# Late modulation columns of a hybrid mixer block: products in column groups of the array in place of sums on the vector engine

## The chip, the cores and the metric

The kernel runs on one core of one Trainium2 chip. A core has five engines that run side by side, each through its own list of instructions in order: TensorE (PE in the profile; its weight loads are shown apart as PEld), VectorE (DVE), ScalarE (ACT), GpSimd (POOL) and SyncE (SP), which here mostly issues DMAs. TensorE writes its results to PSUM, eight banks of 128 partitions by 2 KB; everything else lives in SBUF or in HBM. The metric is the time of one execution on the device in microseconds; lower is better. Beside the timed runs there is one profiled execution, from which all rows of the trace come.

## The reference, cut to what matters

One layer of a diffusion backbone on a latent stream of 1024 tokens by 1024 channels, with a context of 256 tokens. All inputs and the output are float32. A vector `c` of 1024 numbers is turned into six modulation vectors of 1024 numbers, and these scale, shift and gate the stream:

```python
mod = jax.nn.silu(c) @ w_mod[l] + b_mod[l]                    # (1024) @ (1024, 6144)
sh1, sc1, g1, sh2, sc2, g2 = jnp.split(mod[:, None, :], 6, axis=-1)
h = x * (1.0 + sc1) + sh1
z = h @ w_in_l                                                # one input projection, four head groups
y_a = mlstm_mixer(...); y_b = sgu_mixer(...); y_c = conv_mixer(...); y_d = s5_mixer(...)
y = jnp.concatenate([y_a, y_b, y_c, y_d], axis=-1) @ w_out[l]
x = layer_norm(ALPHA * x + g1 * y, ln1_w[l], ln1_b[l])
x = layer_norm(ALPHA * x + g2 * swiglu(x * (1.0 + sc2) + sh2, w_ffn_in[l], w_ffn_out[l]), ln2_w[l], ln2_b[l])
```

The case is about g1, sh2 and sc2, which are columns 2048 to 5119 of `w_mod`: 3072 dot products of length 1024. They are needed late: g1 at the output projection, sh2 and sc2 after the first layer norm.

## The kernel before, in words

The program is written as a straight sequence of operations on tiles. Tiles come from pools; a tile's tag names a slot (or a ring of slots) that tiles share one after another, and a tile can take its slot only when the one before it has been read for the last time. When the program is built, a planner puts the instructions of each engine in one fixed order: what is written earlier goes first, unless a model of durations says that it would have to wait, in which case later work that is ready is put ahead. A few operations are marked as of high priority. On the chip each engine then keeps to its list; an instruction that waits holds up all behind it on its engine, and a DMA that waits for its slot holds up the DMAs behind it on SP's list.

The stages are, in the order written: sh1 and sc1 and the modulated streams; the S5 mixer; projections for the other mixers, each as three passes of a split float32 product (line 884, and line 893 with 256 columns); the mLSTM mixer, whose states (line 487) and eight chunks (lines 531 to 578) pass small products between TensorE, ScalarE and VectorE; the convolution's taps, a long list of VectorE operations (lines 673 to 681); the gating mixer (lines 647 to 653); the convolution's norms (lines 691 to 702); the output projection in two halves of 512 tokens (line 1184); the first layer norm with transposes (line 1204); and the feed-forward layer in seven products of half size instead of eight (lines 1345 and 1470), which takes the second half of the time. Splits of weights into two parts take ScalarE (line 854) and VectorE (line 855).

The six groups of 512 late columns come from `mod_late` (line 975): groups 0 to 2 are written after the first half of the mLSTM, groups 3 to 5 after the first half of the output projection. For a group, `mod_acc` (line 962) loads eight tiles of 128 rows by 512 columns of `w_mod` (line 966, on SP's list), and VectorE adds each, scaled by the matching entry of silu(c) per partition, to an accumulator of 128 partitions by 512 (lines 970 and 968). That leaves one partial sum per partition. Four float32 products of the accumulator with a column of ones (line 981) add over the partitions and put the 512 results into a 128x4 block, to which the bias is added (line 982). The PSUM bank for it is the one bank of tag c, which the gating mixer and the convolution's norms use too. In groups 0 to 2 the accumulator takes the slot of tag kxc, and the weight tiles go in turn through the slots vxc and mw; kxc and vxc are free once the mLSTM's states are made. In groups 3 to 5 the accumulators take kxc and vxc, and the weight tiles go through four parts of the slot vx, which is free after the last mLSTM chunk.

The results of groups 0 and 1 become g1 (lines 1119 to 1125), spread over all partitions by a product; those of groups 2 to 5 are sh2 and sc2 (line 1137 and lines 1219 to 1221). g2 has its own sum (line 1254) and is not touched.

Of the kernel before, what the change touches and what calls it, by code (L numbers as in the profile page):

```python
# [9 lines left out]
F32 = mybir.dt.float32  # L10
# [4 lines left out]
MUL, ADD, SUB, MAX, MIN = ALU.mult, ALU.add, ALU.subtract, ALU.max, ALU.min  # L15
# [4 lines left out]
def bc(ap, shape):  # L20
    return ap.to_broadcast(shape)
# [684 lines left out]
D = 1024  # L706
# [14 lines left out]
def layout(x):  # L721

    f = np.ascontiguousarray
    g = {n: f(x[n]) for n in ("x", "w_mod", "b_mod", "ln1_w", "ln1_b", "ln2_w", "ln2_b", "mlstm_gate_bias", "s5_glu_w")}
    g["cst"] = const_table()
    kp = lambda a: a.reshape(-1, 128).T
    g["cols"] = f(np.concatenate([kp(x["c"]), kp(x["c_ctx"])] + [kp(x[src][0])[:, k0:k0 + nk] for _, src, k0, nk in VEC], 1))

    st = lambda a: a[0].reshape(2, 8, 2, 64).transpose(2, 3, 0, 1).reshape(128, 16)
    ldt = np.broadcast_to(x["s5_log_dt"][0][:, :, None], (2, 16, 64))[None]  # L730
    bt = [x["s5_b_" + n][0].reshape(8, 2, 64, 16).transpose(1, 2, 0, 3).reshape(128, 128) for n in ("re", "im")]
    ct = [x["s5_c_" + n][0].reshape(8, 2, 16, 64).transpose(1, 3, 0, 2).reshape(128, 128) for n in ("re", "im")]
    dk = np.zeros((128, 8), np.float32)
    dk[0:32] = x["s5_d"][0].reshape(8, 32).T
    g["s5p"] = f(np.concatenate([st(x["s5_a_re"]), st(x["s5_a_im"]), st(ldt)] + bt + ct + [dk], 1))
    g["conv_t"] = f(x["conv_w"][0].reshape(31, 2, 128).transpose(2, 1, 0))
    g["sgu_wt"] = f(x["sgu_w"][0].transpose(2, 0, 1))
    g["sgu_bb"] = f(np.repeat(x["sgu_b"][0].reshape(2, 2, 128).transpose(1, 0, 2), 64, 0))
    g["xt"], g["ct"] = (f(x[n][0].T.reshape(8, 128, -1).transpose(1, 0, 2)) for n in ("x", "ctx"))
    tile_ = lambda w: w.reshape(-1, 128, w.shape[1]).transpose(1, 0, 2)  # L740
    half = lambda w: f(np.stack([tile_(w[0:512]), tile_(w[512:1024])]))
    wi = x["w_in"][0]
    g["wt"] = f(np.stack([tile_(wi[:, c:c + 128]) for _, c in TCOLS]))
    g["wk"], g["wb"] = half(wi[:, 256:512]), half(wi[:, 1296:1552])
    g["wv"] = half(np.concatenate([wi[:, 512:768], wi[:, 1024:1040]], 1))
    g["wm"] = f(x["w_mod"][0][:, 0:2 * D].reshape(4, 2, 128, 2, 2, 512).transpose(4, 0, 2, 1, 3, 5))
    blocks = lambda w: f(w.reshape(8, 128, -1, 128).transpose(2, 1, 0, 3))
    g["w1"] = blocks(x["w_ffn_in"][0])
    g["wo"] = f(x["w_out"][0].reshape(4, 2, 128, 2, 512).transpose(3, 0, 2, 1, 4))
    g["w2"] = f(x["w_ffn_out"][0].reshape(NFF // 2, 2, 128, 2, 512).transpose(1, 3, 2, 0, 4).reshape(4, 128, NFF // 2, 512))  # L750
    g["w2k"] = f(x["w_ffn_out"][0].reshape(NFF // 2, 2, 128, 2, 512).transpose(0, 2, 1, 3, 4).reshape(NFF // 2, 128, 4, 512))
    return g
# [10 lines left out]
def body(tc, A, out):  # L763
    nc = tc.nc
    v, a, pe, gp = nc.vector, nc.scalar, nc.tensor, nc.gpsimd
    e = Env()
    e.nc, e.tc = nc, tc
    st = ExitStack()
    with st:
        cp = st.enter_context(tc.tile_pool(name="const", bufs=1))  # L770
# [9 lines left out]
        ld = nc.sync.dma_start  # L780
# [22 lines left out]
        ccol = cp.tile([128, 16], F32, name="ccol")  # L803
# [7 lines left out]
        mx = tc.alloc_tile_pool(name="mx", bufs=1, side="right")  # L811
# [135 lines left out]
        kxc = mx.tile([128, 2, 256], F32, name="kxc", tag="kxc")  # L947
# [14 lines left out]
        def mod_acc(acc, wt, c0):  # L962
            n = acc.shape[-1]
            for k in range(8):
                w = wt()
                ld(w, wm[k * 128:(k + 1) * 128, c0:c0 + n])
                if k:
                    v.scalar_tensor_tensor(acc, w, ccol[:, k:k + 1], acc, op0=MUL, op1=ADD)
                else:
                    v.tensor_scalar(acc, w, ccol[:, k:k + 1], None, op0=MUL)  # L970
# [1 line left out]

        m2c = cp.tile([128, 24], F32, name="m2c")

        def mod_late(groups, acc_, wt, tag):
            for i in groups:
                acc = acc_()
                mod_acc(acc, wt, (4 + i) * 512)
                ps = e.ps(tag)
                for j in range(4):  # L980
                    pe.matmul(ps[:, j:j + 1], lhsT=acc[:, j * 128:(j + 1) * 128], rhs=e.one, start=True, stop=True)
                v.tensor_tensor(m2c[:, i * 4:i * 4 + 4], ps[:, 0:4], col["b2"][:, i * 4:i * 4 + 4], op=ADD)


# [32 lines left out]
        for j in range(2):  # L1017
            ps = ps_mm()
# [78 lines left out]
        def sgu_half(hf):  # L1097
# [3 lines left out]
        chunks(0)  # L1101
        y["a"] = latT(page2([128, 2, 1024]), "o", AF.Sigmoid)
        norms(0)
        mq = iter(range(99))
        mod_late(range(0, 3), lambda: mx.tile([128, 512], F32, name="macc", tag="kxc"),
                 lambda: mx.tile([128, 512], F32, name="mw", tag=("vxc", "mw")[next(mq) % 2]), "c")

        y["b"] = latT(page2([128, 2, 1024]), "u", AF.Gelu_apprx_tanh)
        gv = page2([128, 8, 256])
# [103 lines left out]
        out_proj(0)  # L1213
        mw = mx.tile([128, 4, 512], F32, name="vx", tag="vx")
        ms = iter(range(32))
        ma = iter(("kxc", "vxc") * 2)
        mod_late(range(3, 6), lambda: mx.tile([128, 512], F32, name="macc", tag=next(ma)), lambda: mw[:, next(ms) % 4], "c")

        v.scalar_tensor_tensor(s2, sc2, 1.0, col["l1w"], op0=ADD, op1=MUL)
        v.scalar_tensor_tensor(b2, sc2, 1.0, col["l1b"], op0=ADD, op1=MUL)  # L1220
# [352 lines left out]
```

## Time and profile before

| | us |
|---|---|
| median of 3 runs | 1174.7 |
| lowest, highest | 1173.6, 1176.86 |
| profiled execution | 1174.02 |
| its span, first to last instruction | 1172.2 |

Rows of the trace give times in us from the start of the span. A row of a timeline has start, duration, engine, line, operation, the tiles out<-in, the shape, and how many instructions of that kind are merged (x12); what stands in brackets is idle time just ahead of it, and what ended it. For a product the shape is rows\*columns of the stationary operand, then partitions x columns of the moving one. The duration of a product reaches to its modelled end, and products overlap, so the pace is read from one start to the next. A row of who waited for whom has the total wait in us and how many times. A row of busy time by stretch has the length, then the busy us and count of PE, PEld, DVE, ACT and POOL, the granted clock of TensorE as a share of full speed, the share of the DMA engines, and GB/s.

### The profile page before, as it was taken

Reading aid. Unit: us, or ns where it says so; the run is one execution under the profiler, and the core shown is the slowest. Engines: PE = TensorE matmul, PEld = TensorE weight load, DVE = VectorE, ACT = ScalarE, POOL = GpSimd, SP = SyncE. Lnnn points to the kernel's source line nnn. Section 1 sums busy time; section 2 is a strip of 40 time slices with the busy share of each in tenths; the row PEclk is TensorE's granted clock in tenths of the full one; section 3 lists DMA queues with packets and bytes.
Section 4 is the critical chain, followed back from the end, with each engine's and each line's share of the span. In section 5 each row is a group of like instructions: output and inputs, shape, how many; then the busy total and the mean of one; then the engine's idle time right before and its main releaser. Section 6 shows DMA issues by size and latency. Waiting matters only on the chain.

```text
span 1172.2 us, 15295 instructions
## 1 busy us (share of the span) xinstructions
PE 1133.1 (97%) x5671; PEld 895.4 (76%) x5671; DVE 930.0 (79%) x1851; ACT 445.6 (38%) x691; POOL 9.6 (1%) x30
## 2 busy tenths in 40 slices
PE   6999999999999999989999999999999999999996
PEld 1487788667888788868887888888887778888884
DVE  6588999978899889879968676777778767766775
ACT  1454444522326433582233332333232336433431
POOL 0010000000000000000000000000000000000000
PEclk9999999999999999999999999999999999999998
DMA  9542111022143346362333545345445679766621
GB/s 359 212 133 89 42 46 57 27 71 70 57 141 109 99 157 212 99 225 73 108 123 112 196 179 180 134 153 192 170 154 202 255 259 349 238 196 220 195 103 72
DMA packets 63147, 177.87 MB, mean 152 GB/s; under 512 B 5537, under 2 KB 9793, under 8 KB 61282
## 3 DMA queue, kind: packets, MB, share of 16 engines
q1 hardware_dynamic: 62658, 175.93, 43.3%
q8 instruction: 44, 0.72, 0.3%
q0 software_dynamic: 272, 0.70, 0.2%
q10 hardware_dynamic: 144, 0.29, 0.1%
q14 instruction: 29, 0.24, 0.1%
HBM read 136.54 MB, written 40.35 MB: 151 GB/s over the span
## 4 chain that ended last, share of the span: by engine, by line
PE 77%; DVE 13%; DMA 4%; issue 4%; ACT 2%; POOL 0%; DVEq 0%; ACTq 0%; POOLq 0%
PE mm L1345 16%; PE mm L884 13%; PE a L1345 8%; PE mm L1470 6%; PE mm L1184 4%; PE b L1345 4%; PE b L884 4%; PE a L1470 3%; PE b L1470 3%; PE mm L893 3%; PE c L1470 2%; PE b L564 1%; DVE whl L855 1%; DVE pg L855 1%; DMA raw<-in_w_dram 1%
## 5 line engine op out<-in xcount | busy, mean ns | idle before, releaser
L854 ACT CAST whl<-raw 128x512 fp32r<-128x512 f32 (+1 forms) x198 | 120.3, 622 | 283.2 <-PE mm L884 69.6
L884 PE MATMUL mm<-pg,whl 128*128 128x512 f32 x816 | 217.7, 406 | 1.4 <-ACT pg L1207 1.2
L1345 PE MATMUL mm<-pg,whl 128*128 128x512 f32 x864 | 205.9, 390 | 0.4 <-DVE whl L855 0.3
L1345 PEld LDWEIGHTS mm<-pg,whl 128*128 128x128 f32 x864 | 161.9, 188 | 35.6 <-issue 0.8
L884 PEld LDWEIGHTS mm<-pg,whl 128*128 128x128 f32 x816 | 147.7, 190 | 38.8 <-issue 6.1
L855 DVE TENSOR_TENSOR whl<-raw,whl 128x512 fp32r<-128x512 f32 (+1 forms) x198 | 133.6, 689 | 46.3 <-ACT whl L854 44.7
L1345 PE MATMUL a<-pg,whl 128*128 128x512 f32 x432 | 104.7, 390 | 3.6 <-ACT whl L854 3.6
L1345 PEld LDWEIGHTS a<-pg,whl 128*128 128x128 f32 x432 | 80.7, 188 | 21.3 <-ACT whl L854 4.8
L855 DVE TENSOR_TENSOR pg<-raw,pg 128x1024 fp32r<-128x1024 f32 (+1 forms) x52 | 59.6, 1149 | 20.8 <-ACT pg L854 20.7
L855 DVE TENSOR_TENSOR pg<-whl,pg 128x1024 fp32r<-128x1024 f32 (+1 forms) x42 | 47.4, 1133 | 31.9 <-ACT pg L854 31.6
L854 ACT CAST pg<-raw 128x1024 fp32r<-128x1024 f32 (+1 forms) x52 | 51.5, 992 | 48.9 <-DMA raw<-in_w_dram 18.0
L854 ACT CAST pg<-whl 128x1024 fp32r<-128x1024 f32 (+1 forms) x42 | 41.1, 980 | 65.9 <-PE c L1470 25.2
L893 PE MATMUL mm<-whl,pg 128*128 128x256 f32 (+1 forms) x448 | 63.1, 288 | 0.0
L893 PEld LDWEIGHTS mm<-whl,pg 128*128 128x128 f32 x448 | 58.1, 190 | 1.5 <-issue 1.1
L1345 PE MATMUL b<-pg,whl 128*128 128x512 f32 x216 | 51.9, 389 | 0.0
L1184 PE MATMUL mm<-pg 128*128 128x512 f32 x192 | 50.8, 409 | 0.0
L1184 PE MATMUL mm<-whl,pg 128*128 128x512 f32 x192 | 50.2, 398 | 0.3 <-DVE pg L1172 0.3
L1470 PE MATMUL mm<-pg,pg 128*128 128x512 f32 x171 | 48.0, 389 | 0.0
L1470 PE MATMUL a<-pg,pg 128*128 128x512 f32 x162 | 47.2, 390 | 0.2 <-DVE hs L1484 0.2
L1470 PE MATMUL b<-pg,pg 128*128 128x512 f32 x162 | 47.1, 389 | 0.0
L1345 PEld LDWEIGHTS b<-pg,whl 128*128 128x128 f32 x216 | 40.5, 188 | 8.4
L1184 PEld LDWEIGHTS mm<-pg 128*128 128x128 f32 x192 | 37.4, 198 | 8.6 <-DVE pg L855 0.7
(468 smaller groups left out, 1838.2 us busy)
## 6 DMA issues: line engine op xcount, KB each, us to landing
raw<-in_w_dram SPq DMA_DIRECT2D x59, 512.0 KB
gd<-pg SPq DMA_DIRECT2D x22, 1024.0 KB
whl<-gd SPq DMA_DIRECT2D x35, 512.0 KB
pg<-in_w2k_dram SPq DMA_DIRECT2D x11, 1024.0 KB
td<-pg SPq DMA_DIRECT2D x11, 1024.0 KB
raw<-td SPq DMA_DIRECT2D x20, 512.0 KB
pg<-in_wm_dram SPq DMA_DIRECT2D x16, 512.0 KB
raw<-in_wo_dram SPq DMA_DIRECT2D x16, 512.0 KB
```

What stands on the lines that cost most here:

```text
L564: pe.matmul(ps[:, x * 65:(x + 1) * 65], lhsT=D[d][:, x], rhs=vx[:, h, :], start=True, stop=True)
L854: a.copy(hi, r)
L855: v.tensor_tensor(lo, r, hi.bitcast(F32), op=SUB)
L884: pe.matmul(ps[h], lhsT=W(wi, k), rhs=rhs(hi, h, k), **f)
L893: pe.matmul(ps, lhsT=lhs(hi, k), rhs=Ws[k // 4](wi, k % 4), start=(k == 0 and n == 0), stop=(k == 7 and n == 2))
L1184: pe.matmul(ps, lhsT=Yr(hi, half, k)[:, t * 128:(t + 1) * 128], rhs=Ws[k // 2](wi, k % 2), start=(i + n == 0), stop=(i == 7 and n == 2))
L1345: pe.matmul(ps, lhsT=W[:, wi, k, :], rhs=B[b][hi][:, k], start=(first and k + n == 0), stop=(k == 3 and n == 2), skip_group_check=True)
L1470: pe.matmul(ps[t], lhsT=Ag[:, hi, k, t * 128:(t + 1) * 128], rhs=Bg[:, wi, k], start=(first and k0 + k + m == 0), stop=(k0 + k == NK - 1 a ...
```

## The change

`mod_late` no longer sums on VectorE. The weights are laid out anew on the host: `wm2[i * 4 + x, n]` holds, for column block x of 128 columns of group i, four row blocks of 128 rows (rows n \* 512 to n \* 512 + 511) side by side, so that a load is again 128 partitions by 2 KB. Each load feeds four float32 products: row block g uses its 128 entries of silu(c), repeated over 32 columns, as the stationary operand, the 128x128 weights as the moving one, and writes 32 equal rows to partitions 32g to 32g + 31 of a PSUM bank of tag c. The two loads n = 0 and 1 of a column block add up there. After eight loads the bank holds four partial sums, each repeated over 32 partitions, for 512 columns. ScalarE copies it to SBUF, and four products with the column `gsum` add over the partitions, as the ones did before. `gsum` is 1 in partitions 0, 32, 64 and 96 and 0 elsewhere, made by one VectorE operation out of the identity; it picks one of each 32 equal rows.

The weight tiles of groups 0 to 2 go in turn through kxc, vxc and mw; those of groups 3 to 5 through the four parts of vx as before. The accumulators are gone. `mod_acc` stays for g2.

```diff
@@ layout
+    g["wm2"] = f(x["w_mod"][0][:, 2 * D:5 * D].reshape(2, 4, 128, 24, 128).transpose(3, 0, 2, 1, 4))
@@ body
-        def mod_late(groups, acc_, wt, tag):
+        gsum = cp.tile([128, 1], F32, name="gsum")
+
+        def mod_late(groups, wt, tag):
+
             for i in groups:
-                acc = acc_()
-                mod_acc(acc, wt, (4 + i) * 512)
                 ps = e.ps(tag)
-                for j in range(4):
-                    pe.matmul(ps[:, j:j + 1], lhsT=acc[:, j * 128:(j + 1) * 128], rhs=e.one, start=True, stop=True)
+                for x in range(4):
+                    for n in range(2):
+                        w = wt()
+                        ld(w, A["wm2"][i * 4 + x, n])
+                        for g in range(4):
+                            pe.matmul(ps[g * 32:(g + 1) * 32, x * 128:(x + 1) * 128], lhsT=bc(ccol[:, n * 4 + g:n * 4 + g + 1], [128, 32]),
+                                      rhs=w[:, g], start=(n == 0), stop=(n == 1))
+                z = e.tmp([128, 512], "hs")
+                a.copy(z, ps)
+                ps = e.ps(tag)
+                for x in range(4):
+                    pe.matmul(ps[:, x:x + 1], lhsT=z[:, x * 128:(x + 1) * 128], rhs=gsum, start=True, stop=True)
                 v.tensor_tensor(m2c[:, i * 4:i * 4 + 4], ps[:, 0:4], col["b2"][:, i * 4:i * 4 + 4], op=ADD)
@@ groups 0 to 2
-        mq = iter(range(99))
-        mod_late(range(0, 3), lambda: mx.tile([128, 512], F32, name="macc", tag="kxc"),
-                 lambda: mx.tile([128, 512], F32, name="mw", tag=("vxc", "mw")[next(mq) % 2]), "c")
+        v.tensor_reduce(gsum, e.ident[:, 0:128:32], axis=mybir.AxisListType.X, op=ADD)
+        mq = itertools.cycle(("kxc", "vxc", "mw"))
+        mod_late(range(0, 3), lambda: mx.tile([128, 4, 128], F32, name="mw", tag=next(mq)), "c")
@@ groups 3 to 5
-        ma = iter(("kxc", "vxc") * 2)
-        mod_late(range(3, 6), lambda: mx.tile([128, 512], F32, name="macc", tag=next(ma)), lambda: mw[:, next(ms) % 4], "c")
+        mod_late(range(3, 6), lambda: mw[:, next(ms) % 4].rearrange("p (g c) -> p g c", g=4), "c")
```

## The prediction

> **What bounds the kernel now.** I read the page first, then the busy time by stage around the two places that the change touches, then TensorE's instructions in order of time there, because a busy share alone does not say whether the engine could take more.
>
> ```profile
> span 1172.2 us, 15295 instructions
> ...
> PE 1133.1 (97%) x5671; PEld 895.4 (76%) x5671; DVE 930.0 (79%) x1851; ACT 445.6 (38%) x691; POOL 9.6 (1%) x30
> ...
> PE 77%; DVE 13%; DMA 4%; issue 4%; ACT 2%; POOL 0%; DVEq 0%; ACTq 0%; POOLq 0%
> ```
>
> TensorE (PE) is the engine that is busy nearly always, and 77% of the chain that ends last runs over it. VectorE (DVE) is second. The next view is the busy time in four stretches that hold all of the late modulation.
>
> ```profile
> core 0: us, PE busy (x) PEld busy (x) DVE busy (x) ACT busy (x) POOL busy (x), PEclk, DMA share, GB/s
> 225.00:305.00 80.00, 78.82 (x515) 58.59 (x509) 67.06 (x195) 22.32 (x41) 0.54 (x1) 0.98 0.20 67
> 305.00:365.00 60.00, 59.21 (x368) 52.78 (x367) 55.91 (x117) 20.98 (x31) 0.00 (x0) 1.00 0.28 90
> 365.00:420.00 55.00, 52.58 (x366) 40.87 (x366) 45.56 (x134) 27.16 (x38) 0.00 (x0) 0.94 0.39 135
> 420.00:480.00 60.00, 59.48 (x286) 48.14 (x285) 56.92 (x104) 24.83 (x33) 0.00 (x0) 1.00 0.56 178
> ```
>
> Both engines are nearly full here: DVE 56 of 60 us in the second stretch and 57 of 60 in the fourth. Which of them sets the end is read from TensorE's rows in order of time (start, duration, engine, line, operation, tiles, shape, count).
>
> ```profile
> 318.77 9.79 PE L884 MATMUL mm<-pg,whl 128*128 128x512 f32 x42
> 328.82 0.63 PE L600 MATMUL b<-cst,msq 128*128 128x128 f32 x4 [0.26 <-DVE msq L596]
> ...
> 435.20 2.89 PE L1184 MATMUL mm<-pg 128*128 128x512 f32 x12
> 437.93 2.88 PE L1184 MATMUL mm<-whl,pg 128*128 128x512 f32 x12
> 440.65 2.88 PE L1184 MATMUL mm<-pg 128*128 128x512 f32 x12
> 443.37 2.88 PE L1184 MATMUL mm<-whl,pg 128*128 128x512 f32 x12
> 446.09 2.88 PE L1184 MATMUL mm<-pg 128*128 128x512 f32 x12
> 448.81 0.95 PE L981 MATMUL c<-oz,macc 128*128 128x1 f32 x8
> 449.62 0.71 PE L1184 MATMUL mm<-whl,pg 128*128 128x512 f32 x2
> ```
>
> From 435.20 to 448.81 us there are 60 wide matmuls, 0.227 us each, without a gap; from 318.77 to 328.82 there are 42, 0.239 us each. So TensorE is saturated by its own work in 305 to 365 and 420 to 480 us, though DVE is nearly as full. What is added to TensorE there is added to the end; what DVE is spared helps only where TensorE waits for DVE. The waits of TensorE, in the stretches 305:365, 365:420 and 420:500 in turn, are few:
>
> ```profile
> PE c L981 <- DVE macc L968: 0.5, 1, 0.5
> ...
> PE b L564 <- DVE mD L548: 1.6, 1, 1.6
> PE c L647 <- DVE gwl L650: 0.9, 1, 0.9
> ...
> PE c L981 <- DVE macc L968: 0.2, 1, 0.2
> ```
>
> **What is removed.** The sums of the late modulation are 48 VectorE instructions.
>
> ```profile
> L968 DVE SCALAR_TENSOR_TENSOR macc<-mw,ccol,macc x21: 733/744/754, 256.3 to 346.9; 128x512 f32<-128x512 f32 x21
> L968 DVE SCALAR_TENSOR_TENSOR macc<-vx,ccol,macc x21: 734/746/752, 432.6 to 472.4; 128x512 f32<-128x512 f32 x21
> L970 DVE TENSOR_SCALAR macc<-mw,ccol x3: 477/478/486, 254.8 to 332.7; 128x512 f32<-128x512 f32 x3
> L970 DVE TENSOR_SCALAR macc<-vx,ccol x3: 480/482/483, 427.5 to 457.9; 128x512 f32<-128x512 f32 x3
> ```
>
> 42 x 0.745 + 6 x 0.48 = 34.2 us leave DVE, 17 in each half. Nearly all of it lies under a full TensorE. On the path are the waits of the column sums, 0.5 + 0.2 = 0.7 us, which I count as gained. Indirectly, the first 17 us let the convolution's taps end earlier, so that DVE answers sooner in 365 to 420 us. There the two waits make 1.6 + 0.9 = 2.5 us, and the granted clock of 0.94 over 55 us costs 3.3 us, together 5.8. The lower bound is nothing. I take 3, about half, since most of that stretch is a chain between engines and not a queue on DVE.
>
> **What is added on TensorE.** Each of six groups gets 4 column blocks x 2 halves of the rows x 4 column groups = 32 float32 matmuls (stationary 128x32, moving 128x128), so 48 blocks of four that each need one load. The column sums by 128x1 products stay as they are (8 records, 448.81 to 449.62). A float32 matmul leaves two records in this trace (four column sums stand as 8). No row has four column groups, so I use the nearest: the same shape in one group (L231), and two groups of 64 columns (L487, L691).
>
> ```profile
> 65.08 0.62 PE L231 MATMUL b<-s5V,s5BD 128*32 128x128 f32 x4
> ...
> 263.78 0.48 PE L884 MATMUL mm<-pg,whl 128*128 128x512 f32 x1
> 264.19 0.45 PE L487 MATMUL b<-vx,mke 128*64 128x65 f32 x8
> 264.58 0.98 PE L884 MATMUL mm<-pg,whl 128*128 128x512 f32 x3
> ...
> 269.94 0.69 PE L487 MATMUL b<-vx,mke 128*64 128x65 f32 x16
> ...
> 381.50 1.09 PE L691 MATMUL c<-cst,ap 128*64 128x128 f32 x16
> 382.52 2.79 PE L1184 MATMUL mm<-whl,pg 128*128 128x512 f32 x11
> ```
>
> In L231 four records in one group end 0.62 us after they start, of which the page gives the last 0.27: (0.62 - 0.27) / 3 = 0.117, so I take 0.11 us a record, the end of the stream being modelled. In L691 sixteen records of the same moving width, in two groups, take 1.02 us; one after another they would take 16 x 0.11 = 1.76. So two groups run side by side. The change of mode costs as well: from 263.78 to 264.58 one wide matmul and eight L487 records take 0.80 us. Less 0.227 that is 0.57, and eight more records cost 0.69 - 0.45 = 0.24, so 0.33 us is paid for going into and out of the small form. One block of four matmuls alone then costs 2 x 0.11 + 0.33 = 0.55 us if four groups run together, 4 x 0.11 + 0.33 = 0.77 if two do, 8 x 0.11 + 0.33 = 1.21 if none do. I take four, because two already overlap fully in L691.
>
> The Trainium skill's TensorEngine Tiling (Array Packing), section Key Properties, says that changing the tiling mode drains the engine; the 0.33 us agrees. Its TensorE: Matmul & The Clock Gate, section Measured speedup vs the span model, gives 2.38x for three column groups. If four groups reached in proportion an estimated 4 x 2.38 / 3 = 3.2x, a block's inner time would be 0.88 / 3.2 = 0.275 in place of 0.22 us, and the sum 2.6 us larger.
>
> How many blocks run alone follows from the loads. The loads are issued by SyncE (SP) in these trains:
>
> ```profile
> 255.29 15.73 SPq L966 DMA_DIRECT2D mw<-in_w_mod_dram  x6
> ...
> 331.44 8.65 SPq L966 DMA_DIRECT2D mw<-in_w_mod_dram  x5
> ...
> 433.36 11.98 SPq L966 DMA_DIRECT2D vx<-in_w_mod_dram  x10
> ```
>
> They come 1.2 to 2.6 us apart, many wide matmuls, so a block finds no neighbour unless it waits for one. All alone: 48 x 0.55 = 26.4. Each group in one run: 6 x (16 x 0.11 + 0.33) = 12.5. I take half the blocks alone and half in pairs: 24 x 0.55 + 12 x 0.77 = 22.4 us. 48 loads of 256 KB stay 48 of 256 KB, on the same queue.
>
> **What is moved.** The wait for a weight tile moves from DVE to TensorE, whose matmuls behind it then wait too (L884, L893, L1184). DVE's waits for these loads were this, from the row of who waited for L966:
>
> ```profile
>   DVE macc L968: 1.4, 4
> ```
>
> I charge the same 1.4 us to TensorE; nothing is the lower end, and the upper is below. Loads behind a weight tile on SP's queue are now freed by TensorE. Six copies of 128x512 from PSUM go to ACT, which is busy 21 of 60 and 25 of 60 us; DVE's slack and TensorE's other work hide them, and uncovered they would be about 6 x 0.6 = 3.6 us by the eviction at L1057 below. Each copy holds one of the two hs slots through which L1188 and L1189 pass the output projection's rows; the other slot keeps these going, so I cost it at nothing. The one bank c is now held while a group's eight loads arrive, ahead of the sums. Its other users, the convolution's norms, end at 434.53, before the second half's first column sums at 448.81.
>
> ```profile
> 326.56 0.60 ACT L1057 ACTIVATE pg<-mm 128x512 f32<-128x512 f32 x1
> ...
> 434.53 0.60 PE L700 MATMUL c<-cst,cxn 128*128 128x128 f32 x4
> ```
>
> **Sum.** +22.4 - 0.7 - 3 + 1.4 = +20.1 us. The profiled execution took 1174.02 us (span 1172.2 and 1.8 around it), 0.7 below the median of 1174.7; 1174 + 20 = 1194.
>
> **Rivals.**
> A, the forecast: four groups side by side, switching paid, TensorE the bound. 1194; by runs of blocks (12.5 to 26.4) and the DVE gain (0 to 5.8) its own range is 1181 to 1201. Chance 0.58.
>
> B, two groups at a time, or late weights. With 0.77 a block: 48 x 0.77 = 37, so 1174 + 37 - 2.3 = 1209. If all 48 blocks met a late load as those four did, 48 x 0.35 = 17 in place of 1.4, also about 1209. For the first: only pairs are shown; for the second: TensorE runs in order. Against: L691's clean pairs, and only 4 of 48 loads were late. Chance 0.16.
>
> C, no overlap of groups: 48 x 1.21 = 58, so 1230. L691 speaks against it. Chance 0.05.
>
> ```profile
> L487 PE MATMUL b<-vx,mke 128*64 128x65 f32 x112 | 6.1, 233 | 0.0
> ...
> L487 PE MATMUL b<-vxc,mke 128*64 128x65 f32 x32 | 1.8, 234 | 0.0
> ```
>
> D, the other side: DVE is what holds TensorE back from 225 to 420 us. Its place is the chains of small matmuls and VectorE steps (L487, L548, L564). With DVE freed, the small matmuls bunch: the 144 records at L487, 18 runs of eight, paired as at 269.94 save 9 x 0.33 = 3.0 us, the four chunks after 365 us as much again, plus the whole 5.8 and the clock of 0.98 over 80 us, 1.6: 13.4 us. With each group's blocks in one run, 12.5 - 0.7 - 13.4 = -1.6, so 1172; it decides once the gains pass the 12 us that TensorE must take at the least. For it: DVE at 93 to 95%. Against: the same rows of wide matmuls without gaps. Chance 0.15.
>
> E, TensorE has room that its busy share hides: PEld is busy only 48 of 60 us in 420:480. If the 20% free could take the blocks, only the gains are left: 1174 - 0.7 - 3 = 1170. The Trainium skill's Trainium Kernel Development and Optimization, section Performance Expectations, calls matmul busy time a bad metric and weight-load busy time a good one; by that rule this is the outcome. Against it stand 60 wide matmuls at an even 0.227 us. Chance 0.06.
>
> **Numbers.** Predicted 1194. The range reaches down to D and up past B: 1172 to 1213; outside are C, E and the rims of D and B, about 0.2. Faster by more than 0.3% (3.5 us, about what a measurement here can tell from no change): E and about half of D, 0.13. Within 0.3%: the rest of D, 0.09. Slower: A, B and C, 0.78. Nearly all the chance is on one side, so the range stands alone.
>
> **What would show it.** In the changed profile: the new line's records on bank c, four starting within hundredths of a us and the next four 0.11 us later (A), or pairs (B), or singles (C); its runs, mostly of 8 to 16 records, each followed by a wide matmul about 0.3 us later than the records account for. The stretch from the first to the last of each half should hold the same wide matmuls in some 10 us more, with DVE's busy share down by 17 us a half. TensorE's waits for in_wm2 loads should sum to a few us. I am wrong if wide matmuls between the blocks keep their count per us (E), or if the stretch 365 to 420 us shrinks by more than 6 us (D).

## The result and the profile after

The changed kernel takes 1212.0 us, the median of 4 runs (1210.4 to 1213.3); the kernel before, run beside it, 1175.65 us (1173.6 to 1176.9). The ratio is 1.031, 95% interval 1.029 to 1.0331: 36.4 us slower. The forecast was slower by 20, 1194 us, with a range of 1172 to 1213. The sign was right and the time lies at the upper rim of the range.

The page of the changed kernel (span, busy time by engine, shares of the chain of waits by engine):

```profile
span 1210.3 us, 15983 instructions
...
PE 1168.9 (97%) x6055; PEld 905.2 (75%) x6055; DVE 903.9 (75%) x1804; ACT 449.9 (37%) x697; POOL 9.6 (1%) x30
...
PE 84%; DVE 8%; DMA 4%; ACT 2%; issue 1%; SPq 0%; DVEq 0%; POOL 0%; ACTq 0%; POOLq 0%
```

VectorE is busy 26 us less (930.0 to 903.9), TensorE 36 us more, and TensorE's share of the chain went from 77% to 84%. The lines after the change lie a little lower: 893 is now 894, 1184 is 1196, 1345 is 1356; the new products are line 987 and the column sums line 993.

TensorE's rows of the changed kernel in order of time (start, duration, engine, line, operation, tiles, shape, count), first from the first half of the late modulation, then from the second:

```profile
318.73 0.86 PE L987 MATMUL c<-mw,ccol 128*32 128x128 f32 x24
...
322.01 0.42 PE L987 MATMUL c<-mw,ccol 128*32 128x128 f32 x8
322.37 0.73 PE L885 MATMUL mm<-pg,whl 128*128 128x512 f32 x2
323.03 0.42 PE L987 MATMUL c<-mw,ccol 128*32 128x128 f32 x8
...
463.44 1.08 PE L987 MATMUL c<-vx,ccol 128*32 128x128 f32 x32
...
468.44 0.43 PE L987 MATMUL c<-vx,ccol 128*32 128x128 f32 x8 [1.21 <-DMA vx<-in_wm_dram]
468.80 0.97 PE L1196 MATMUL mm<-whl,pg 128*128 128x512 f32 x3
469.69 0.42 PE L987 MATMUL c<-vx,ccol 128*32 128x128 f32 x8
470.05 0.73 PE L1196 MATMUL mm<-whl,pg 128*128 128x512 f32 x2
470.71 0.42 PE L987 MATMUL c<-vx,ccol 128*32 128x128 f32 x8
```

One block of four products is eight records. Three blocks take 0.86 us, four 1.08, one 0.42: each further block costs (1.08 - 0.42) / 3 = 0.22 us; that the four column groups run side by side there is shown below against a run with one group. From 322.01 to 323.03 lies one block and two wide matmuls of 0.227 us: 1.02 - 0.22 - 0.454 = 0.35 us is paid for going into and out of the small form, and from 469.69 to 470.71 the same. Read off all rows of this view, the 48 blocks fall into 20 runs in the first half and 17 in the second. So the new line costs 48 x 0.22 + 37 x 0.35, about 23.5 us.

Where the whole difference lies is read from the same instructions in both kernels: rows of one line, whose last numbers before the forms are the starts of its first and its last instruction. Before:

```profile
L893 PE MATMUL mm<-whl,pg x448: 277/283/396, 78.1 to 363.9; 128*128 128x256 f32 x75, 128*128 128x272 f32 x75
...
L1184 PE MATMUL mm<-pg x192: 387/389/774, 396.9 to 496.3; 128*128 128x512 f32 x192
...
L1345 PE MATMUL mm<-pg,whl x864: 388/389/497, 598.8 to 947.2; 128*128 128x512 f32 x173
...
L1345 PE MATMUL b<-pg,whl x216: 389/389/390, 607.0 to 939.0; 128*128 128x512 f32 x108
```

After:

```profile
L894 PE MATMUL mm<-whl,pg x448: 278/283/396, 80.2 to 379.4; 128*128 128x256 f32 x75, 128*128 128x272 f32 x75
...
L1196 PE MATMUL mm<-pg x192: 387/389/736, 412.4 to 523.7; 128*128 128x512 f32 x192
...
L1356 PE MATMUL mm<-pg,whl x864: 388/389/497, 628.5 to 982.8; 128*128 128x512 f32 x173
...
L1356 PE MATMUL b<-pg,whl x216: 395/396/397, 636.8 to 974.4; 128*128 128x512 f32 x108
```

| stretch | before, us | after, us | longer by |
|---|---|---|---|
| start to the first of L893 / L894 | 78.1 | 80.2 | 2.1 |
| to the last of it (first half of the modulation) | 285.8 | 299.2 | 13.4 |
| to the last of L1184 / L1196 (second half) | 132.4 | 144.3 | 11.9 |
| to the first of L1345 / L1356 | 102.5 | 104.8 | 2.3 |
| to the last of it | 348.4 | 354.3 | 5.9 |
| to the end of the span | 225.0 | 227.5 | 2.5 |

The two stretches that hold the new products make 25.3 of the 38.1 us between the two profiled executions. The fifth, in the feed-forward layer, was touched by nothing in the diff's arithmetic, and is 5.9 us longer: its b rows go from 389 to 396 ns. The three small ones sum to 6.9 us; the experiments return to both.

### The profile page after: what moved, and what is told of

It is laid out like the page before. It is cut to its first block, busy times and chain, and to the rows that moved or that the text cites. A ratio compares the mean times of both kernels' runs of the same rounds, so it can differ in the third digit from the quotient of the medians.

```text
span 1210.3 us, 15983 instructions
## 1 busy us (share of the span) xinstructions
PE 1168.9 (97%) x6055; PEld 905.2 (75%) x6055; DVE 903.9 (75%) x1804; ACT 449.9 (37%) x697; POOL 9.6 (1%) x30
## 4 chain that ended last, share of the span: by engine, by line
PE 84%; DVE 8%; DMA 4%; ACT 2%; issue 1%; SPq 0%; DVEq 0%; POOL 0%; ACTq 0%; POOLq 0%
PE mm L1356 16%; PE mm L885 15%; PE a L1356 8%; PE mm L1481 6%; PE mm L1196 5%; PE a L1481 5%; PE b L1356 4%; PE b L1481 4%; PE b L885 4%; PE mm L894 3%; PE c L1481 2%; DMA pg<-in_wm_dram 2%; PE b L564 1%; DVE whl L856 1%; PE c L987 1%
## 5 line engine op out<-in xcount | busy, mean ns | idle before, releaser
L885 PE MATMUL mm<-pg,whl 128*128 128x512 f32 x816 | 223.6, 410 | 1.4 <-ACT pg L1219 1.2
L1356 PE MATMUL mm<-pg,whl 128*128 128x512 f32 x864 | 208.0, 392 | 0.2 <-DVE whl L856 0.2
L1356 PEld LDWEIGHTS mm<-pg,whl 128*128 128x128 f32 x864 | 162.2, 188 | 37.6 <-ACT whl L855 0.7
L1356 PE MATMUL a<-pg,whl 128*128 128x512 f32 x432 | 107.4, 396 | 3.6 <-ACT whl L855 3.6
L1356 PEld LDWEIGHTS a<-pg,whl 128*128 128x128 f32 x432 | 80.8, 188 | 23.9 <-ACT whl L855 4.8
L856 DVE TENSOR_TENSOR pg<-whl,pg 128x1024 fp32r<-128x1024 f32 (+1 forms) x42 | 47.4, 1133 | 31.8 <-ACT pg L855 28.1
L855 ACT CAST pg<-whl 128x1024 fp32r<-128x1024 f32 (+1 forms) x42 | 40.9, 977 | 66.4 <-PE c L1481 25.3
L894 PE MATMUL mm<-whl,pg 128*128 128x256 f32 (+1 forms) x448 | 62.9, 288 | 0.0
L894 PEld LDWEIGHTS mm<-whl,pg 128*128 128x128 f32 x448 | 58.1, 190 | 1.5 <-issue 1.1
L1196 PE MATMUL mm<-pg 128*128 128x512 f32 x192 | 53.6, 413 | 0.9 <-DVE pg L856 0.6
L1356 PE MATMUL b<-pg,whl 128*128 128x512 f32 x216 | 53.3, 396 | 0.0
L1196 PE MATMUL mm<-whl,pg 128*128 128x512 f32 x192 | 50.9, 399 | 0.0
L1356 PEld LDWEIGHTS b<-pg,whl 128*128 128x128 f32 x216 | 40.6, 188 | 9.6
L1481 PE MATMUL a<-pg,pg 128*128 128x512 f32 x162 | 47.4, 391 | 0.2 <-DVE hs L1495 0.2
L1196 PEld LDWEIGHTS mm<-pg 128*128 128x128 f32 x192 | 35.7, 194 | 11.2 <-issue 2.4
```

The lines of the kernel that those rows point to most:

```text
L855: a.copy(hi, r)
L856: v.tensor_tensor(lo, r, hi.bitcast(F32), op=SUB)
L885: pe.matmul(ps[h], lhsT=W(wi, k), rhs=rhs(hi, h, k), **f)
L894: pe.matmul(ps, lhsT=lhs(hi, k), rhs=Ws[k // 4](wi, k % 4), start=(k == 0 and n == 0), stop=(k == 7 and n == 2))
L1196: pe.matmul(ps, lhsT=Yr(hi, half, k)[:, t * 128:(t + 1) * 128], rhs=Ws[k // 2](wi, k % 2), start=(i + n == 0), stop=(i == 7 and n == 2))
L1356: pe.matmul(ps, lhsT=W[:, wi, k, :], rhs=B[b][hi][:, k], start=(first and k + n == 0), stop=(k == 3 and n == 2), skip_group_check=True)
```

## The experiments

Each kernel below is timed against the kernel before on the same chip. "Without the shift" means the first one.

**The new small tile moves the big ones.** `gsum` holds one float per partition, but in the pool it takes 32 bytes, and every pool placed behind it (pg, whl, pg2, raw, hs) begins 32 bytes higher than before; pg3, placed from the other end, stays. The feed-forward products of the lengthened stretch read weights in whl, 864 of 1512 (four in each seven products) against a moving operand in pg3. The first experiment is the changed kernel with `gsum` in bytes that were unused:

```diff
-        oz = cp.tile([128, 2], F32, name="oz")
+        oz = cp.tile([128, 3], F32, name="oz")
-        gsum = cp.tile([128, 1], F32, name="gsum")
+        gsum = oz[:, 2:3]
```

> The changed kernel, but gsum is put into the unused bytes of the slot of the ones column, so that no tile behind it moves by 32 bytes. In the changed kernel's trace the feed-forward's wide products with the moving operand in the third page pool and weights in the pools that moved start 235 ns apart in the middle, those whose operands moved together 227. Theory P (the 32-byte move of the pools costs the pace): all of these return to 227 ns, the first-to-last time of the seven feed-forward products of the first kind falls from 354 to about 348 us, and the whole is 7 to 9 us faster than the changed kernel, near 1.024 of before. Rival Q (another chip or another execution, or the new products themselves): the pace stays at 230 to 235 ns and the ratio at 1.031.

Measured: 1202.0 us (1201.8 to 1203.0), ratio 1.0226 [1.0198, 1.0255], some 10 us below the changed kernel (1.031 - 1.0226 = 0.0084 of 1175). Its rows by line:

```profile
L894 PE MATMUL mm<-whl,pg x448: 274/283/401, 78.3 to 376.7; 128*128 128x256 f32 x75, 128*128 128x272 f32 x75
...
L1196 PE MATMUL mm<-pg x192: 387/389/775, 409.7 to 520.3; 128*128 128x512 f32 x192
...
L1356 PE MATMUL mm<-pg,whl x864: 387/389/628, 622.1 to 973.9; 128*128 128x512 f32 x173
...
L1356 PE MATMUL b<-pg,whl x216: 389/389/390, 630.3 to 965.7; 128*128 128x512 f32 x108
```

The b rows are back at 389 ns. The first half is 298.4 us, 12.6 longer than before, the second 143.6, 11.2 longer: 23.8 us for the change without the shift. The feed-forward stretch, though, is 351.8 us, not the 348 that I expected. The products of pg3 are back at 227 ns in most of it. The excess lies in a few places; in the largest TensorE waits 2.0 us for a split of weights, and then starts some ten wide products only every 0.43 us, at a granted clock of 0.66 from 955 to 960 us. In the five other kernels below that have new products and no shift, this stretch takes 347.9 to 348.7 us.

**The shift alone, without the change.** The kernel before with `oz` nine columns wide instead of two, which puts the same pools 32 bytes higher and changes no instruction.

```diff
-        oz = cp.tile([128, 2], F32, name="oz")
+        oz = cp.tile([128, 9], F32, name="oz")
```

> The kernel before with the ones column's slot made 32 bytes longer, so that all tiles written behind it in the left pools move by 32 bytes, as in the changed kernel; the instructions and their order are the same. Theory P: wide products with the moving operand in the third page pool go from 227 to 230 to 235 ns, and the kernel is 7 to 9 us slower than before, ratio about 1.007. Rival Q: the same time as before, ratio 1.000, all at 227 ns.

Measured: 1182.4 us, ratio 1.0054 [1.0034, 1.0073]. The rows of line 1345:

```profile
L1345 PE MATMUL mm<-pg,whl x864: 388/389/497, 597.7 to 951.9; 128*128 128x512 f32 x173
...
L1345 PE MATMUL b<-pg,whl x216: 395/396/397, 606.0 to 943.6; 128*128 128x512 f32 x108
```

354.2 us instead of 348.4: the 5.9 us of the changed kernel, made by a tile that nobody reads. The spacing of the products of pg3 with whl goes from 227 to 231-235 ns; the other three in each seven, those of pg and pg2 with whl, whose two operands were moved together, stay at 227.

**Place or distance?** The next one leaves the left pools where they were and moves pg3 alone, 32 bytes down:

```diff
-        g2 = pg3.tile([128, D], F32, name="g2", tag="g2", bufs=1)
+        g2 = pg3.tile([128, D + 8], F32, name="g2", tag="g2", bufs=1)[:, 0:D]
```

> The kernel before, with the third page pool alone moved down by 32 bytes; the left pools, with the weights, stay where they were. Theory R (what counts is whether moving operand and weights start at the same offset within 64 bytes): the same wide products as with the left pools moved, moving operand in the third page pool and weights in the left pools, go from 227 to 230 to 235 ns, and the kernel is 5 to 8 us slower than before, ratio 1.005 to 1.007. Rival S (what counts is where the weights or the left pages start by themselves): they stay at 227 ns, ratio 1.000, or get faster.

Measured: 1183.9 us, ratio 1.0078 [1.0055, 1.0102].

```profile
L1345 PE MATMUL mm<-pg,whl x864: 387/389/499, 600.9 to 955.5; 128*128 128x512 f32 x173
```

354.6 us with whl at its old address. Either operand of these products, moved alone, slows them, and products whose operands move together stay as they were, so it is the distance between the two that counts. Both moves bring the operands closer by 32 bytes; the other direction was not tried. Then how much distance is harmless, by more columns in `oz` of the kernel before (17, 33 and 65 instead of two, that is 64, 128 and 256 bytes):

> The kernel before, with the small tile oz made 17 columns wide instead of 1, so that the pools behind it (pg, whl, pg2, raw, hs) lie 64 bytes higher, and pg3 where it was; instructions and their order unchanged. If what costs time is an offset of 32 bytes, odd or even, between moving operand and weights, 64 bytes leave it as it was: wide products of pg3 and whl at 227 ns, ratio 1.000 (0.998 to 1.002). If it is the absolute place of whl, or steps of 128 bytes that count, they stay at 231 to 235 ns and the ratio is 1.005 to 1.010, as with 32 bytes.

Measured: 1184.3 us, ratio 1.0079 [1.0049, 1.011].

```profile
L1345 PE MATMUL mm<-pg,whl x864: 387/389/499, 598.4 to 952.5; 128*128 128x512 f32 x173
```

> The kernel before with oz 33 columns wide, so that pg, whl, pg2, raw and hs lie 128 bytes higher and pg3 where it was; instructions and order unchanged. Shifts of 32 and of 64 bytes between pg3 and whl both took the wide products from 227 to 231-235 ns. If the distance counts modulo 128 bytes, 128 bytes leave it as before: 227 ns, 265 to 267 wide products in each 60 us from 640 to 880 us, ratio 1.000 (0.998 to 1.002). If any move away from the old place costs, or the step is 256 bytes or more, 261 or 262 products and a ratio of 1.005 to 1.010.

Measured: 1182.3 us, ratio 1.0063 [1.0044, 1.0083].

```profile
L1345 PE MATMUL mm<-pg,whl x864: 387/389/501, 600.4 to 954.1; 128*128 128x512 f32 x173
```

> The kernel before with oz 65 columns wide, so that pg, whl, pg2, raw and hs lie 256 bytes higher and pg3 where it was; instructions and order unchanged. 32, 64 and 128 bytes each took the wide products of pg3 and whl from 227 to 231-235 ns; before, their addresses agree modulo 256 bytes. If the distance counts modulo 256 bytes, 256 bytes leave it as before: 227 ns, 265 to 267 wide products in each 60 us from 640 to 880 us, ratio 1.000 (0.998 to 1.002). If any move from the old place costs, 261 or 262 products and a ratio of 1.005 to 1.010.

Measured: 1174.1 us, ratio 0.9992 [0.9974, 1.0009].

```profile
L1345 PE MATMUL mm<-pg,whl x864: 388/389/499, 597.9 to 946.4; 128*128 128x512 f32 x173
...
L1345 PE MATMUL b<-pg,whl x216: 389/389/389, 606.1 to 938.2; 128*128 128x512 f32 x108
```

The stretch is 354.1 us at 64 bytes, 353.7 at 128 and 348.5 at 256. My first two guesses at the step, 64 and then 128 bytes, were wrong; of the distances tried, 0 and 256 bytes cost nothing, and 32 (whichever operand is moved), 64 and 128 cost 5.3 to 6.2 us here and 6.4 to 9.3 us in the whole time. At 64 bytes the slowed products start 231 to 235 ns apart, at 128 bytes 229 to 238. Why the chip does so is not known from these runs.

**Half of the change at a time**, both without the shift: groups 0 to 2 as products and 3 to 5 as VectorE's sums, and the other way round. The core of the first:

```diff
-        mod_late(range(3, 6), lambda: mw[:, next(ms) % 4].rearrange("p (g c) -> p g c", g=4), "c")
+        ma = iter(("kxc", "vxc") * 2)
+        mod_late0(range(3, 6), lambda: mx.tile([128, 512], F32, name="macc", tag=next(ma)), lambda: mw[:, next(ms) % 4], "c")
```

> Without the 32-byte move; groups 0 to 2 as products in column groups, groups 3 to 5 as VectorE sums as before. If the cost is TensorE time per block (about 0.22 us and 0.33 us for each run's going in and out), the first half alone costs 11 to 13 us: 24 x 0.22 + 19 runs x 0.33 = 11.5, plus 1.1 us of waits for loads, less 1 to 3 us from VectorE. Ratio about 1.010. If VectorE's sums had held up the stretch 365 to 420 us, more than 5 us would come back there and the ratio would be under 1.006.

> Without the 32-byte move; groups 0 to 2 as VectorE sums as before, groups 3 to 5 as products in column groups. By the price per block: 24 x 0.22 + 17 runs x 0.33 = 10.9, plus up to 5.5 us of TensorE's waits for weight loads, about 14 us, ratio about 1.012. If the waits for loads are hidden by other waits, 11 us, ratio 1.009. With the first half's 11 to 13 the two should add to what the changed kernel without the move shows, within 2 us; if not, the halves disturb one another.

Measured: 1187.4 us, ratio 1.0104 [1.0072, 1.0135], with 20 runs; and 1188.75 us, ratio 1.0115 [1.0081, 1.0149], with 17 runs. The two sum to 1.0219 against 1.0226 for both together: within these intervals neither half does anything for the other, and each costs what its blocks and runs do (24 x 0.22 + 20 x 0.35 = 12.3 us against 12.2; 24 x 0.22 + 17 x 0.35 = 11.2 against 13.5, whose interval reaches down to 9.5).

**VectorE's sums taken away, with nothing put on TensorE.** The kernel before with all 48 late loads, but only the last of each eight summed, so that the late modulation comes from an eighth of its weights:

```diff
-                mod_acc(acc, wt, (4 + i) * 512)
+                for k in range(8):
+                    w = wt()
+                    ld(w, wm[k * 128:(k + 1) * 128, (4 + i) * 512:(5 + i) * 512])
+                    if k == 7:
+                        v.tensor_scalar(acc, w, ccol[:, k:k + 1], None, op0=MUL)
```

> The kernel before, with all 48 late weight loads kept, but only the last of each eight summed by VectorE: 42 of the 48 sums are left out, about 30 of the 34 us that the change takes off VectorE, so the late modulation comes from an eighth of its weights. Nothing is added on TensorE. If VectorE held TensorE back there, the time falls by 3 us (the forecast's own term) up to 13 us or more (the rival in which VectorE sets the pace): ratio 0.997 down to 0.989. If the sums were hidden throughout, it stays: ratio 0.999 to 1.001, 0 to 1 us.

Measured: 1173.85 us, ratio 0.9992 [0.9978, 1.0007]. Its busy time by stage (columns: the stretch, its length, then busy time and count of PE, PEld, DVE, ACT and POOL, TensorE's granted clock, DMA share, GB/s) and, below, what TensorE waits for from 365 to 420 us:

```profile
305.00:365.00 60.00, 60.00 (x387) 53.00 (x386) 40.62 (x95) 23.39 (x35) 0.00 (x0) 1.00 0.15 45
...
420.00:480.00 60.00, 59.39 (x276) 48.09 (x275) 47.36 (x94) 28.20 (x37) 0.00 (x0) 1.00 0.48 153
```

```profile
PE b L564 <- DVE mD L548: 1.6, 1, 1.6
PE c L647 <- DVE gwl L650: 0.9, 1, 0.9
```

VectorE goes from 55.9 to 40.6 us of 60 in the first of these stretches and from 56.9 to 47.4 in the second, TensorE stays full, and the two waits in the convolution's stretch are the same to a tenth. The 42 sums were worth 0.9 us at the median, with 2.6 at the most by the interval.

**All four products in one column group.** The changed kernel without the shift, each block's four products written one after another to the same 32 rows, of which the copy and the column sums then take 32 partitions only:

```diff
-                            pe.matmul(ps[g * 32:(g + 1) * 32, x * 128:(x + 1) * 128], lhsT=bc(ccol[:, n * 4 + g:n * 4 + g + 1], [128, 32]),
-                                      rhs=w[:, g], start=(n == 0), stop=(n == 1))
+                            pe.matmul(ps[0:32, x * 128:(x + 1) * 128], lhsT=bc(ccol[:, n * 4 + g:n * 4 + g + 1], [128, 32]),
+                                      rhs=w[:, g], start=(n + g == 0), stop=(n == 1 and g == 3))
```

> The changed kernel without the 32-byte move, but all four products of a load go to the first column group, where all eight loads of a group add up; the column sums then read 32 partitions. The same products, weights and loads, without groups side by side. If four groups run at once in the changed kernel (its rows show four starts within 0.02 us and the next four 0.11 us or less later), a block's inner time goes from 0.20 to 8 x 0.11 = 0.88 us, and the kernel gets slower by 48 x 0.66 = 32 us, to about 1.049 of before. Rival: the price of a block is its going in and out of the small form and the groups save little; then the kernel is slower by less than 10 us, under 1.031.

Measured: 1227.9 us, ratio 1.045 [1.0426, 1.0473]: 26 us over the kernel without the shift, less than expected. TensorE's rows:

```profile
317.73 2.81 PE L987 MATMUL c<-mw,ccol 128*32 128x128 f32 x24
...
324.12 1.06 PE L987 MATMUL c<-mw,ccol 128*32 128x128 f32 x8 [0.26 <-DMA mw<-in_wm_dram]
```

24 records take 2.81 us where four groups took 0.86; (2.81 - 1.06) / 16 = 0.109 us a record, 0.88 a block, four times 0.22. That is the forecast's third rival, C, made on purpose. Over 48 blocks it makes 48 x 0.66 = 32 us more, and most of the difference to 26 is the switching that I had left as it was: the runs fall from 37 to 14, which saves 23 x 0.35 = 8 us. (The likely reason is that slower blocks find the next weights already there.) The 2 us between 24 and 26 are not told apart.

**The loads taken away.** The changed kernel without the shift, 41 of the 48 loads left out (the first three and the first four tiles are used again and again):

```diff
...
-                        ld(w, A["wm2"][i * 4 + x, n])
+                        if nl < nw:
+                            ld(w, A["wm2"][i * 4 + x, n])
+                        nl += 1
...
```

> The changed kernel without the 32-byte move, but only the first three weight tiles of groups 0 to 2 and the first four of groups 3 to 5 are loaded, and all products use these tiles again: 41 of the 48 loads are left out, and the late modulation is computed from the wrong weights. If TensorE's waits for weight tiles, 6.3 us in the profile without the move, are on the path, the kernel is 5 to 7 us faster than without the move, ratio 1.017 to 1.018. If they only take the place of other waits, 0 to 2 us, ratio 1.021 to 1.023. As blocks need not wait for a load, they may also bunch, which would be worth 0.33 us for each run saved, up to 10 us more; the number of runs in the trace tells the two apart.

Measured: 1187.2 us, ratio 1.0112 [1.009, 1.0134].

```profile
315.31 1.95 PE L989 MATMUL c<-mw,ccol 128*32 128x128 f32 x64
...
322.86 1.95 PE L989 MATMUL c<-mw,ccol 128*32 128x128 f32 x64
```

The blocks of a group stand in one run of 64 records, six runs in all. 48 x 0.22 + 6 x 0.35 = 12.7 us; the ratio makes 13.2. So this is the forecast's lower end, 12.5 us with each group in one run, and with all loads the kernel takes 13.4 us more (26.6 by the ratio of the first experiment): 31 more runs x 0.35 make 11 of it. Of the other 2.5, TensorE's waits for these loads are 1.2 in the first experiment's profile; the rest is within the intervals.

**Fewer and larger loads.** If the trickle costs, four tiles in one load of 1 MB should bring the runs of the second half from 17 to some 6. The changed kernel without the shift, groups 3 to 5:

```diff
-        mod_late(range(3, 6), lambda: mw[:, next(ms) % 4].rearrange("p (g c) -> p g c", g=4), "c")
...
+                w4 = mx.tile([128, 4, 4, 128], F32, name="vx", tag="vx")
+                ld(w4, A["wm2"][i * 4 + xx * 2:i * 4 + xx * 2 + 2].rearrange("x n p g c -> p (x n) g c"))
...
```

> The changed kernel without the 32-byte move, but groups 3 to 5 load four weight tiles in one DMA of 1 MB into one slot, so that blocks come in runs of four. If going in and out of the small form costs 0.33 us a run, 6 runs in place of 17 save 11 x 0.33 = 3.6 us; with only one slot the loads can come late, which costs TensorE nothing as long as it has other work ahead of them. Expected 2 to 5 us faster than without the move, ratio 1.018 to 1.021. If the price lies in the products themselves and not in the switch, no change, 1.0226.

Measured: 1211.0 us, ratio 1.03 [1.0265, 1.0335], 9 us slower than with small loads, where I had expected 2 to 5 faster. TensorE's rows, then its waits for these loads from 440 to 520 us and the busy time of five microseconds behind the longest:

```profile
492.32 1.08 PE L1235 MATMUL c<-vx,ccol 128*32 128x128 f32 x32 [2.50 <-DMA vx<-in_wm_dram]
499.06 1.94 PE L1235 MATMUL c<-vx,ccol 128*32 128x128 f32 x32 [5.66 <-DMA vx<-in_wm_dram]
501.75 1.86 PE L1241 MATMUL c<-oz,hs 128*128 128x1 f32 x8 [0.76 <-ACT hs L1238]
503.48 5.04 PE L1196 MATMUL mm<-whl,pg 128*128 128x512 f32 x12
```

```profile
PE c L1235 <- DMA vx<-in_wm_dram: 10.0, 3, 5.7
```

```profile
499.00:504.00 5.00, 4.18 (x41) 3.59 (x42) 0.35 (x2) 0.59 (x1) 0.00 (x0) 0.50 0.00 0
```

There are only five runs, but the one slot is free for the next load only when its four tiles have been used, and TensorE, which keeps to its list, waits for it, 10.0 us in three waits, with wide matmuls of the output projection still behind them. Behind them it is slow as well: the granted clock is 0.50 from 499 to 504 us, against 1.00 from 435 to 475, the four blocks from 499.06 take 1.94 us instead of 1.08, and the 12 wide matmuls 0.42 us each instead of 0.227. By the count of runs the switching should have fallen by 12 x 0.35 = 4 us; the waits and the slow clock behind them took more than that. Two slots of 1 MB were not tried.

## Why the prediction was right, and where it was too small

**What bounds the kernel**: right. TensorE was full, and what was put on it came out at the end. The rival E, that TensorE's busy share hides room, would have left the two stretches as long as they were; they grew by 25.3 us. The Trainium skill's Trainium Kernel Development and Optimization, section Performance Expectations, which names weight-load busy time and not matmul busy time as a good metric, would have led astray here: PEld at 75-76% looked like room, and there was none. One reading was a little off: the 0.239 us for the 42 matmuls from 318.77 us takes in the idle time behind them; from start to start they are 0.229 us apart.

**Added on TensorE**: right in each part. Four groups side by side with 0.22 us a block: measured 0.22. Switching 0.33: measured 0.35. About 36 runs (24 single blocks and 12 pairs): 37, but that is partly luck, since there were no pairs; a few runs of three and four blocks made up for more single ones. 22.4 us forecast, 23.5 by the rows. The rivals with two groups at a time or none (the first kind of B, and C) fall: the rows above, and the run that made C on purpose. The estimate of 0.275 us a block from the Trainium skill's TensorE: Matmul & The Clock Gate, section Measured speedup vs the span model, was too high: four groups gave 0.88 / 0.22 = 4.0 times one, not the 3.2 carried over from its three (its figure is for 512 columns of moving data, these products have 128).

**What is removed**: mis-sized. The step took 3 us, about half of 5.8, for VectorE answering sooner from 365 to 420 us. The changed kernel's waits of TensorE from 380 to 435 us:

```profile
PE b L564 <- DVE mD L548: 1.6, 1, 1.6
PE c L647 <- DVE gwl L650: 0.9, 1, 0.9
```

They are the rows of before, word for word, and leaving out 42 of the 48 sums brought 0.9 us at the median. The stretch is a chain between the engines, as the forecast itself said, and no run shows VectorE's queue having a part in it; the lower bound, nothing, was the value to take. Rival D, in which VectorE holds TensorE back, falls with the same run (it needed 12 us).

The other part of the 5.8 was the clock. In the ten microseconds behind the 1.6 us wait the granted clock was 0.66 before and 0.83 in the changed kernel, 1.7 us less lost. But it was 0.66 without VectorE's sums, and it differs between kernels with the very same instructions, before and the second experiment (columns as above):

```profile
404.60:414.60 10.00, 9.99 (x41) 8.35 (x42) 6.53 (x23) 0.72 (x2) 0.00 (x0) 0.66 0.71 241
```

```profile
403.40:413.40 10.00, 9.99 (x48) 8.34 (x49) 7.91 (x26) 0.72 (x2) 0.00 (x0) 0.83 0.65 237
```

So this is no gain of the change that these runs could show, and a stretch can differ by such an amount between two profiles without a change in the instructions. The 34.2 us were also too many as VectorE's own gain: its busy time fell by 26.1, since busy time counts the overlapping ends of neighbouring instructions once (the late sums overlapped their neighbours by 8.0 us). The 0.7 us of the column sums' waits was gained: TensorE waits nowhere at line 993.

**What is moved**: right within what can be seen. The rows of line 987, and what ended the idle time before them (on weight loads and matmuls together):

```profile
L987 PE MATMUL c<-mw,ccol x192: 272/273/296, 318.7 to 353.6; 128*32 128x128 f32 x192
...
L987 PE MATMUL c<-vx,ccol x192: 272/273/297, 463.4 to 493.2; 128*32 128x128 f32 x192
...
  DMA vx<-in_wm_dram: 5.5, 8
  DMA mw<-in_wm_dram: 1.1, 3
```

The 6.6 us count the weight loads' idle time, which partly lies under matmuls that still run. Of TensorE's own matmuls the view of waits from 435 to 520 us has this:

```profile
PE c L987 <- DMA vx<-in_wm_dram: 1.6, 2, 1.2
```

1.6 us against 1.4 forecast, so the second kind of B, late weights for 17 us, falls too. ScalarE's six copies, the hs slot and bank c, costed at nothing, end no wait of TensorE.

**Sum**: this is the step that failed. With the measured terms the forecast's own sum is 23.5 - 0.7 - 0 + 1.6 = 24.4, and the two stretches that it speaks of grew by 23.8 without the shift and by 25.3 with it; the clock's 1.7 us above is a measure of how closely such figures can agree. What the sum had no term for is the new tile `gsum`: 4 bytes that moved five pools by 32, and made each product of pg3 with whl 4 to 8 ns longer. That is 5.9 us in the one stretch, shown by making the shift alone, by four distances, and by the pace of these products when it is taken away. In whole times it is 6.4 us for the shift alone, and 10 between the changed kernel and the first experiment. Of those 10 only 2.5 lie in this stretch, because the first experiment had its longer waits there (351.8 us); where the others come from isn't known.

**What stays open**: 25.3 + 5.9 is 31.2 of the 38.1 us between the profiled executions. 1.6 of the remaining 6.9 are the profiled execution of before, 1174.0 us, below the median of 1175.65 beside the changed kernel. For the last stretch there are these rows (columns as above), of before, of the changed kernel and of the one without VectorE's sums; each begins at the last product of the feed-forward stretch, and holds the same 926 matmuls:

```profile
947.20:1172.20 225.00, 210.85 (x926) 173.16 (x924) 153.48 (x207) 91.47 (x112) 0.00 (x0) 0.98 0.60 202
```

```profile
982.80:1210.30 227.50, 213.21 (x926) 174.49 (x924) 153.67 (x207) 92.25 (x113) 0.00 (x0) 0.97 0.59 200
```

```profile
947.30:1174.90 227.60, 213.18 (x926) 175.36 (x924) 153.42 (x207) 92.09 (x113) 0.00 (x0) 0.97 0.60 200
```

The kernel without VectorE's sums is as fast as before, has neither new products nor the shift, and takes 227.6 us here, so the last stretch's 2.5 us need not be the change's. In the first experiment's profile the three small stretches together are only 0.6 us longer than before. So the new products hardly explain the 6.9; how much of it is the shift's and how much belongs to the executions compared isn't settled.

That the range held is luck in part: its upper end had been put past rival B, and the time came there for another reason.

No version here beats the kernel before: every block put on TensorE costs time on the engine that sets the end, and the cheapest form tried with all 48 blocks, six runs of 64 records without most of the loads, is still 1.1% slower.

## What to carry to other kernels

Work on an engine that is busy 79% of the time can be free while another is full, as it was here: take it away alone in one run before paying for it elsewhere. Small products on a full TensorE were priced here by how often it goes into and out of them (0.35 us) more than by the products (0.22 us a block), and that count follows from how the loads arrive. A tile of a few bytes can move every pool behind it: compare the addresses of the large operands before and after a change, and keep new constants in space that was already taken.

## What the runs showed that was not expected

Wide products with moving operand and weights in different pools kept a spacing of 227 ns while the pools' distance was changed by 0 or 256 bytes, and went to 231-235 ns at 32 and 64 bytes and to 229-238 at 128, at a granted clock of 1.00 from 640 to 880 us: 5.3 to 6.2 us over 864 products and those beside them, with every instruction the same. Four column groups of 32 gave the full factor of four (0.22 us a block against 0.88 in one group). Slower blocks were partly paid back, 32 us of products costing 26, as the array changes its form 14 times instead of 37. And behind waits of 1.6 us (the kernel before, from 408 to 410 us) and of 5.7 us (the large loads, from 499 to 504 us) TensorE's granted clock was 0.50; after the shorter wait it differed between kernels with the same instructions (0.66 against 0.83 over ten microseconds).
